# A second layer's merges with tokens as the stationary side and 512 weight columns moving, and a new opening

## The chip, the cores and the metric

The kernel runs on one core of a Trainium2 chip. The metric is the device time of one execution in microseconds (us), as a median over repeated runs. A core has engines with instruction streams of their own: PE (TensorE) multiplies matrices, DVE (VectorE), ACT (ScalarE) and POOL (GpSimd) work element by element, and SP (SyncE) issues most of the transfers from HBM. They wait for each other through semaphores.

## The reference

Two layers of a trunk with parallel branches work on 256 tokens x and 256 context tokens, each of 1024 channels. Cut to what matters:

```python
for l in range(2):
    last = l == 1
    mod_x = sc @ w_mod[l] + b_mod[l]     # sc = silu(c); six pieces of 1024
    mod_h = sh @ w_mod[l] + b_mod[l]     # the same for the context, sh = silu(c_ctx)
    ux = rms_norm(x, norm1_g[l]) * (1 + cx1) + sx1
    uh = rms_norm(h, norm1_g[l]) * (1 + ch1) + sh1
    qa, ka, va, qb, kb, vb, pc, gates = project(ux, w_in[l], ...)   # and of uh
    ya = neighborhood_attention(qa, ka, va, ka_h, va_h, rpb_a[l])
    yb = gqa_block_attention(rope(qb), concat(kb_h, rope(kb)), concat(vb_h, vb))
    yc = multiscale_pool(pc, w_pool[l], pool_scale[l])
    g = sigmoid(gates)                   # three pieces of 1024
    m = g[0] * (ya @ w_br_a[l]) + g[1] * (yb @ w_br_b[l]) + g[2] * (yc @ w_br_c[l])
    x = x + gx1 * (m @ w_out[l])
    u2 = rms_norm(x, norm2_g[l]) * (1 + cx2) + sx2
    x = x + gx2 * ((silu(u2 @ w_ff1[l]) * (u2 @ w_ff3[l])) @ w_ff2[l])
    if not last:
        ...                              # the same for the context tokens h
```

All of it is float32. The second layer needs the context tokens only for keys and values, so from its queries on it works with 256 tokens, the first layer with 512. `ya` and `yb` have 384 channels, `yc` has 256.

## The kernel before

**Products.** Each float32 matrix product is done as three products of a shorter format, from a high and a low part of both sides (`mm3`, L224 to L229: high by high, high by low, low by high). A weight tile of 128 rows and up to 512 columns is loaded raw by SP, ACT copies it into the high part `wh` (L133) and DVE subtracts to get the low part `wl` (L145). The class `Weights` holds 7 raw tiles and 6 of each part, and works some tiles ahead of PE in the order of a list that the jobs make. Tiles marked `whole` aren't split; they are multiplied in whole float32. Activations are kept with channels on the partitions (`xT`, `u`, `y`, `m`), so that a product's result has channels on the partitions again: the weights are the stationary side, the tokens move, 512 or, in the second layer, 256 of them at a time.

**Order.** `program` makes a list of jobs from the string `ORDER`, one letter a job (layer 1 first): P pooling, K, Q, N projections for the attentions, a, b and c the merges of the three branches. Each job is a generator that yields after some products, and at each yield the scheduler `Side` makes one step of attention, pooling or normalization work; a number that such a step yields says how many ticks it stays away. Another `Side` spreads the product of the modulation vectors for later (`w_mod`, on DVE) over the kernel. No engine reorders anything: what is written out is each engine's order.

**The merges.** `merge_job` does 256 channels of one branch: it multiplies `u` (`uh`, `ul`) by the gate's columns of `w_in` over 8 channel tiles, ACT makes the tanh, it waits until the branch's `y` is there, multiplies that by the branch's weights (2 or 3 tiles), and `mix` joins gate and sum on DVE. Four such jobs make a branch, twelve a layer. The last branch, a, splits the sum into the parts of `m`, the moving side of `w_out` (`into_job`, through `pair`). In the second layer both parts of such a merge are products with 256 moving columns.

**The pooling.** `pool_job` projects `pc`; `pool_mix` sums windows of it on POOL, step by step, splits the result and multiplies it on PE into `yc`. Before that product stands `yield 4`.

**The opening.** `first_job` is written by hand. Two pieces of the modulation, the shift (m0) and the scale (m2) of the first 512 channels, are products of the two vectors `sf` with 8 + 8 whole tiles of `w_mod` in `mod_first`; x comes in between in two halves, is squared on ACT and turned on PE (`turn_x`). `norm_rstd` sums the squares on PE and makes 1/rms. Then DVE multiplies `xT` by it for four channel tiles and POOL for the other four (`xr`), and `start_u` makes the parts of `u` from `xr`, scale and shift:

```python
for kt in range(KT):
    xr.append(self.g([P, TOK], name="xr"))
    (nc.vector if kt < 4 else nc.gpsimd).tensor_tensor(xr[kt], self.xT[:, kt, :], self.r0, ALU.mult)
    steps(m, 1)
```

Behind it come half of the first projection (na, channel tiles 0 to 3), two split pieces of the modulation (m1, m3: shift and scale of the other channels), half of the pooling's projection, and then the second halves of both.

## Time and profile before

| | |
|---|---|
| median of 3 runs | 1223.53 us (1223.06 to 1224.26) |
| the profiled execution | 1225.7 us, its span 1223.9 us (1.8 us lie around it) |
| mean granted clock of PE | 0.993 of full speed |
| busy share of the span | PE 98%, PE's weight loads 86%, DVE 75%, ACT 52%, POOL 10% |
| instructions in the trace | 20,258 |
| read from HBM | 183.05 MB, 150 GB/s over the span |

The profile is of one execution, taken by the hardware profiler. A busy share says how much of the span the engine had an instruction at work; loads of weights overlap products on PE. The granted clock is the share of full speed at which PE was allowed to run; it has two levels, 1.2 and 2.4 GHz, shown as 0.5 and 1.0. The waits are told by the instruction that waited and the one whose end released it.

### The profile page before, as it was taken

How to read it: one execution, taken by the hardware profiler on the slowest of the kernel's cores; microseconds unless marked ns; L12 is line 12 of the kernel's file. 1: busy time of each engine (PE TensorE's matmuls, PEld its weight loads, DVE VectorE, ACT ScalarE, POOL GpSimd, SP SyncE). 2: the span in 40 equal slices, each digit the busy share in tenths (PEclk: the TensorE clock that was granted, in tenths of full speed). 3: DMA queues.
4: the chain of work that ended last, by engine and by line, in shares of the span. 5: the costliest groups of instructions: out<-in, count | busy, mean ns of one | idle time of the engine just before them, and what ended most of it. 6: DMA issues, size and time to landing. Idle time of an engine off the chain costs nothing.

```text
span 1223.9 us, 20258 instructions
## 1 busy us (share of the span) xinstructions
PE 1196.1 (98%) x7059; PEld 1058.0 (86%) x7059; DVE 921.4 (75%) x1770; ACT 641.6 (52%) x1393; POOL 127.3 (10%) x177
## 2 busy tenths in 40 slices
PE   7899999999999999999999999999999999999998
PEld 2788889788888988888888888999999999999987
DVE  5867789989898996768566764788778878765654
ACT  4655588666433543333222333456877767655542
POOL 3253110201100000000000000153022100000000
PEclk9899999999999999999999999999999999999999
DMA  8632244335464535555556663334344565666563
GB/s 280 219 84 77 69 146 120 98 104 159 129 199 146 181 104 166 162 159 171 195 184 214 204 206 116 86 106 113 91 118 114 149 193 164 199 182 184 163 194 113
DMA packets 157522, 185.44 MB, mean 152 GB/s; under 512 B 12792, under 2 KB 135532, under 8 KB 157420
## 3 DMA queue, kind: packets, MB, share of 16 engines
q1 hardware_dynamic: 155612, 181.49, 48.1%
q0 software_dynamic: 1808, 2.66, 1.8%
q8 instruction: 55, 0.90, 0.3%
q14 instruction: 47, 0.39, 0.1%
HBM read 183.05 MB, written 1.05 MB: 150 GB/s over the span
## 4 chain that ended last, share of the span: by engine, by line
PE 83%; DVE 5%; ACT 4%; DMA 4%; POOL 2%; issue 1%; SPq 1%; ACTq 0%; DVEq 0%; POOLq 0%
PE acc L227 25%; PE acc L228 25%; PE acc L229 25%; PE y L840 2%; DMA whole<-in_w_mod_dram 2%; PE pt L886 1%; DVE wl L145 1%; DMA mraw<-in_w_mod_dram 1%; ACT wh L133 1%; POOL s L1027 1%; ACT p L829 1%; PE s L863 1%; PE s L864 1%; ACT p L831 1%; DMA raw<-in_w_in_dram 1%
## 5 line engine op out<-in xcount | busy, mean ns | idle before, releaser
L133 ACT ACTIVATE wh<-raw 128x512 fp32r<-128x512 f32 (+2 forms) x512 | 307.7, 612 | 348.5 <-PE acc L228 228.6
L145 DVE TENSOR_TENSOR wl<-raw,wh 128x512 fp32r<-128x512 f32 (+2 forms) x512 | 339.1, 670 | 151.5 <-ACT wh L133 147.7
L227 PE MATMUL acc<-uh,wh 128*128 128x512 f32 (+1 forms) x784 | 279.6, 358 | 2.9 <-ACT gate L1098 1.6
L229 PE MATMUL acc<-uh,wl 128*128 128x512 f32 (+1 forms) x784 | 276.8, 354 | 2.4 <-DVE wl L145 2.4
L228 PE MATMUL acc<-ul,wh 128*128 128x512 f32 (+1 forms) x784 | 277.3, 355 | 0.3
L490 DVE SCALAR_TENSOR_TENSOR macc<-mraw,sf,macc 128x1024 f32<-128x1024 f32 x112 | 144.4, 1294 | 51.0 <-DMA mraw<-in_w_mod_dram 50.9
L227 PEld LDWEIGHTS acc<-uh,wh 128*128 128x128 f32 x784 | 148.7, 190 | 23.6 <-ACT gate L1098 2.0
L229 PEld LDWEIGHTS acc<-uh,wl 128*128 128x128 f32 x784 | 148.6, 190 | 22.9 <-DVE wl L145 2.9
L228 PEld LDWEIGHTS acc<-ul,wh 128*128 128x128 f32 x784 | 149.0, 190 | 20.3 <-DVE ul L579 0.7
L227 PE MATMUL acc<-wh,uh 128*128 128x384 f32 (+1 forms) x304 | 99.6, 329 | 5.0 <-ACT uh L1374 4.4
L228 PE MATMUL acc<-wl,uh 128*128 128x384 f32 (+1 forms) x304 | 97.8, 322 | 0.0
L229 PE MATMUL acc<-wh,ul 128*128 128x384 f32 (+1 forms) x304 | 97.7, 322 | 0.0
L227 PE MATMUL acc<-u,wh 128*128 128x256 f32 x320 | 91.3, 286 | 0.0
L229 PE MATMUL acc<-u,wl 128*128 128x256 f32 x320 | 91.0, 285 | 0.0
L228 PE MATMUL acc<-u,wh 128*128 128x256 f32 x320 | 90.5, 283 | 0.0
L227 PE MATMUL acc<-hh,wh 128*128 128x512 f32 (+1 forms) x216 | 75.9, 351 | 0.0
L229 PE MATMUL acc<-hh,wl 128*128 128x512 f32 (+1 forms) x216 | 75.6, 350 | 0.0
L228 PE MATMUL acc<-hl,wh 128*128 128x512 f32 (+1 forms) x216 | 75.5, 350 | 0.0
L227 PEld LDWEIGHTS acc<-wh,uh 128*128 128x128 f32 x304 | 58.5, 192 | 6.5 <-ACT uh L1374 4.5
L227 PEld LDWEIGHTS acc<-u,wh 128*128 128x128 f32 x320 | 61.4, 192 | 0.6 <-issue 0.2
L229 PEld LDWEIGHTS acc<-u,wl 128*128 128x128 f32 x320 | 61.4, 192 | 0.3 <-issue 0.2
L228 PEld LDWEIGHTS acc<-u,wh 128*128 128x128 f32 x320 | 61.4, 192 | 0.2 <-issue 0.2
(289 smaller groups left out, 2317.0 us busy)
## 6 DMA issues: line engine op xcount, KB each, us to landing
raw<-in_w_ff_dram SPq DMA_DIRECT2D x264, 256.0 KB, 3.0
mraw<-in_w_mod_dram SPq DMA_DIRECT2D x80, 512.0 KB, 4.1
raw<-in_w_in_dram SPq DMA_DIRECT2D x112, 256.0 KB, 2.7
raw<-in_w_in_dram SPq DMA_DIRECT2D x144, 64.0 KB, 2.0
whole<-in_w_mod_dram SPq DMA_DIRECT2D x32, 256.0 KB, 5.4
raw<-in_w_out_dram SPq DMA_DIRECT2D x32, 256.0 KB, 2.8
raw<-in_w_in_dram SPq DMA_DIRECT2D x16, 192.0 KB, 2.4
raw<-in_w_br_c_dram SPq DMA_DIRECT2D x8, 256.0 KB, 2.9
```

The costliest lines, as they stand in the source:

```text
L133: self.nc.scalar.activation(hi[:, :n], self.raw[i][:, :n], AF.Copy)
L145: self.nc.vector.tensor_tensor(lo[:, :n], self.raw[i][:, :n], self.hi[i][:, :n].bitcast(F32), ALU.subtract)
L227: mm(out, st[0], mv[0], start=start, stop=False)
L228: mm(out, st[0], mv[1], start=False, stop=False)
L229: mm(out, st[1], mv[0], start=False, stop=stop)
L490: nc.vector.scalar_tensor_tensor(acc[v], w, c, acc[v], ALU.mult, ALU.add)
L829: nc.scalar.activation(pt, ps, AF.Exp, scale=-1.0, bias=m, accum_out=s[:, 0:1])
L831: nc.scalar.activation(pt, pt, AF.Copy, scale=s[:, 1:2])
L840: mm(o, st, t[:, kt % 2, :], start=kt == 0 and i == 0, stop=kt == n - 1 and i == 1)
L863: nc.tensor.matmul(ps, st, ks[h][0], start=True, stop=False)
L864: nc.tensor.matmul(ps, st, ks[h][1], start=False, stop=True)
L886: nc.tensor.transpose(ps[:, kt * P : (kt + 1) * P], pr[h, qt][:, kt * P : (kt + 1) * P], self.ident)
```

## The change

**The second layer's merges** are done by `merge_tok` instead of `merge_job`: the tokens' parts are stationary (128 tokens a product), and 512 columns of the weights move. A job does 512 channels of a branch for both halves of the tokens, so two jobs make a branch and six the layer. The three branch tiles of a job are fetched before the first of their products. The gates and the sum now have tokens on the partitions, and the sum over the branches is made on DVE alone. It is then turned back on PE, four transposes for 128 tokens and 512 channels, in `turn_m`, which is a step of the scheduler; the first products of `w_out` wait, in the written order, for the turns of the channels that they need. `ORDER` of the second layer has two letters for each branch instead of four, and one merge c in another place. `pool_mix` yields 12 instead of 4 ahead of its product in that layer.

**The opening.** 8 of the 16 whole tiles of `mod_first` become split ones (`mod_first` has four whole tiles and then four split ones for each piece), the scale is now made before the shift, and each result has four rows instead of two. `norm_rstd` comes in the middle of the first piece: its product over the squares first, then the splits of that piece's four tiles and their products, and then its steps on DVE and ACT. `xr` and `start_u` are gone: `norm_u`, which serves the other normalizations, makes `u` from `xT`, scale and 1/rms in one step; its first two steps stand ahead of the wait for the shift. Two of the eight copies of `turn_x` go to ACT. Six products of the pooling's projection stand ahead of the wait for the second half's scale. 16 products of 128 columns with ones (`WARM`) stand near the first transpose. The three transfers of an `na` tile become one.

```diff
-ORDER = ("KrcQcNgcNcbbbbaaaa", "tQPNKccNcNcbbbbaaaa")
+ORDER = ("KrcQcNgcNcbbbbaaaa", "tQPNKcNcNbbaa")
...
+WARM = 8
...
         ps = self.u()
+        for _ in range(WARM):
+            nc.tensor.matmul(ps[:, P : 2 * P], self.ones, self.ones, start=True, stop=True)
         nc.tensor.transpose(ps[:, 0 : 2 * KT], sc[0 : 2 * KT, :], self.ident[0 : 2 * KT, 0 : 2 * KT])
+        warm = self.u("warm")
+        for _ in range(WARM):
+            nc.tensor.matmul(warm[:, 0:P], self.ones, self.ones, start=True, stop=True)
...
+            if h == 1 and k > 1:
+                nc.scalar.activation(self.xT[:, 4 * h + k, :], ps, AF.Copy)
+            else:
+                nc.vector.tensor_copy(self.xT[:, 4 * h + k, :], ps)
+            yield
...
-    def mod_first(self, l, j):
+    def mod_first(self, l, j, nw):
...
-            return TOK, [f], "whole"
+            return TOK, [f], "whole" if kt < nw else "far"
...
-                w = get.__self__.get_whole()
-                nc.tensor.matmul(ps[0:2, :], self.sf[:, kt, :], w, start=kt == 0, stop=kt == KT - 1)
+                if kt < nw:
+                    w = get.__self__.get_whole()
+                    nc.tensor.matmul(ps[0:4, :], self.sf4[:, kt].rearrange("p v h -> p (v h)"), w, start=kt == 0, stop=kt == KT - 1)
+                else:
+                    w = get(TOK, 5)
+                    st = self.S[:, 4 * kt : 4 * kt + 4]
+                    for i in range(2):
+                        nc.tensor.matmul(ps[0:4, :], st, w[i][:, 0, :], start=False, stop=kt == KT - 1 and i == 1)
...
-    def norm_u(self, kts, vs):
+    def norm_u(self, kts, vs, ahead=UA, wait=None):
...
+        if wait:
+            yield wait
...
                 if kind == "na":
-                    for s in range(3):
-                        c0 = 384 * s + P * p
-                        q.dma_start(
-                            out=dst[:, :, s * P : (s + 1) * P],
-                            in_=rows[:, c0 : c0 + P].rearrange("(k p) c -> p k c", p=P),
-                        )
+                    src = rows[:, 0:1152].rearrange("p (s c) -> p s c", c=384)[:, :, P * p : P * (p + 1)]
+                    q.dma_start(out=dst[:, 0, :].rearrange("p (s c) -> p s c", c=P), in_=src)
...
-            yield 4
+            yield 4 if l == 0 else 12
             ps = self.u("pool")
...
+    def merge_tok(self, l, br, h):
...
+        def run(get):
+            nc = self.nc
+            ps = [self.acc() for _ in range(2)]
+            sg = [self.g([P, TOK], name="gate") for _ in range(2)]
+            for kt in range(KT):
+                self.need_u(kt, slice(0, SEQ))
+                w = [x[:, 0, :] for x in get(TOK)]
+                for tt in range(2):
+                    self.mm3(ps[tt], [x[:, tt * P : (tt + 1) * P] for x in self.uu[kt]], w, kt == 0, kt == KT - 1)
+                    if kt == KT - 1:
+                        nc.scalar.activation(sg[tt], ps[tt], AF.Tanh, scale=0.5)
+                    yield
+            want = {(l, "x", br, i) for i in range(nk)}
+            self.side.until(lambda: want <= self.done)
+            pb = [self.acc() for _ in range(2)]
+            ws = [[x[:, 0, :] for x in get(TOK, k)] for k in range(nk)]
+            for tt in range(2):
+                for k in range(nk):
+                    st = [x[:, tt * P : (tt + 1) * P] for x in self.y[br, k]]
+                    self.mm3(pb[tt], st, ws[k], k == 0, k == nk - 1)
+                    if k < nk - 1:
+                        yield
+                t = self.g([P, TOK], name="mix")
+                nc.vector.scalar_tensor_tensor(t, sg[tt], 1.0, pb[tt], ALU.add, ALU.mult)
+                if br != "c":
+                    nc.vector.tensor_tensor(t, self.m0[h, tt], t, ALU.add)
+                self.m0[h, tt] = t
+                if br == "a":
+                    self.side.add(self.turn_m(h, tt, t), first=True)
+                yield
...
+    def turn_m(self, h, tt, t):
+
+        yield 2
+        ps = self.u("mt")
+        for c in range(4):
+            self.nc.tensor.transpose(ps[:, c * P : (c + 1) * P], t[:, c * P : (c + 1) * P], self.ident)
...
-    def start_u(self, kts):
...
-            m = m0[1](get)
+            ws._dma(2 * KT + 4)
+            m = m2[1](get)
             steps(m, X0)
             steps(self.turn_x(x0, 0), 9)
             steps(m, X1)
             steps(self.turn_x(x1, 1), 9)
+            ws._dma(4 * KT + 4)
+            self.norm_rstd(slice(0, TOK), lambda: (ws._lo(KT), steps(m, 4)))
             steps(m, 9)
-            m = m2[1](get)
             steps(self.turn_rows, 9)
-            self.norm_rstd(slice(0, TOK))
-            xr = self.xr = []
-            for kt in range(KT):
-                xr.append(self.g([P, TOK], name="xr"))
-                (nc.vector if kt < 4 else nc.gpsimd).tensor_tensor(xr[kt], self.xT[:, kt, :], self.r0, ALU.mult)
-                steps(m, 1)
-                if kt == 3:
-                    ws._lo(ws.n_whole + 4)
+            m = m0[1](get)
+            steps(m, 1)
+            self.side.until(lambda: ("mod", 0, 2) in self.done)
+            steps(m, 3)
+            ws._lo(2 * KT)
+            ws._hi(2 * KT + 1)
+            self.side.add(self.norm_u(range(4), (0, 1), 2, lambda: ("mod", 0, 0) in self.done), first=True)
...
-            self.side.add(self.start_u(range(4)), first=True)
...
             steps(m3[1](get), 99)
+
+            self.side.until(lambda: ("mod", 0, 1) in self.done)
+            steps(p, 1)
             self.side.until(lambda: ("mod", 0, 3) in self.done)
-            self.side.add(self.start_u(range(4, KT)), first=True)
+            self.side.add(self.norm_u(range(4, KT), (0, 1)), first=True)
...
-        return m0[0] + m2[0] + wa[:4] + m1[0] + m3[0] + wp[:2] + wa[4:] + wp[2:], run
+        return m2[0] + m0[0] + wa[:4] + m1[0] + m3[0] + wp[:2] + wa[4:] + wp[2:], run
...
             for br in "abc":
-                made[br] = iter([self.merge_job(l, T, br, jp) for jp in range(4)])
+                if last:
+                    made[br] = iter([self.merge_tok(l, br, h) for h in range(2)])
+                else:
+                    made[br] = iter([self.merge_job(l, T, br, jp) for jp in range(4)])
```

In the opening, on DVE, from the first `xr` of before and from the first piece of the modulation in the change (`ut` is `xT` by scale and 1/rms, `modt` the turned result of a piece, `whole` and `raw` are weight tiles as loaded). Before:

```order
L1415 TENSOR_TENSOR xr_336<-xT,rstd_117 128x512
L1415 TENSOR_TENSOR xr_339<-xT,rstd_117 128x512
L1415 TENSOR_TENSOR xr_342<-xT,rstd_117 128x512
L449 COPY mod_110<-modt_345 128x8
L453 TENSOR_TENSOR mod_110<-mod_110,cols_109 128x8
L145 TENSOR_TENSOR wl_354<-raw_190,wh_352 128x384
L145 TENSOR_TENSOR wl_358<-raw_194,wh_356 128x384
L145 TENSOR_TENSOR wl_362<-raw_198,wh_360 128x384
L145 TENSOR_TENSOR wl_366<-raw_202,wh_364 128x384
L449 COPY mod_110<-modt_382 128x8
L453 TENSOR_TENSOR mod_110<-mod_110,cols_109 128x8
L519 SCALAR_TENSOR_TENSOR A_111<-mod_110,cols_109 128x8
```

And with the change:

```order
L469 TENSOR_REDUCE mod_130<-modt_366 128x8
L471 TENSOR_TENSOR mod_130<-mod_130,cols_129 128x8
L537 SCALAR_TENSOR_TENSOR A_131<-mod_130,cols_129 128x8
L146 TENSOR_TENSOR wl_379<-whole_202,wh_377 128x512
L146 TENSOR_TENSOR wl_383<-whole_204,wh_381 128x512
L146 TENSOR_TENSOR wl_387<-whole_206,wh_385 128x512
L146 TENSOR_TENSOR wl_391<-whole_208,wh_389 128x512
L590 SCALAR_TENSOR_TENSOR ut_395<-xT,A_131,rstd_137 128x256
L590 SCALAR_TENSOR_TENSOR ut_397<-xT,A_131,rstd_137 128x256
L146 TENSOR_TENSOR wl_399<-raw_210,wh_393 128x384
L469 TENSOR_REDUCE mod_130<-modt_411 128x8
L471 TENSOR_TENSOR mod_130<-mod_130,cols_129 128x8
```

The scale `A` stood behind the four `xr` and the four splits of the projection's weights; it now stands ahead of the four splits of the second piece, two `ut` stand ahead of the shift's reading, and no `xr` is left.

On PE, at the same place in the program, the gate part of a merge early in the second layer: the accumulators are `acc`, the moving side stands first behind the arrow and the stationary side second, `uh` and `ul` are parts of `u`, `kt` is a transpose of the attention's keys. Before:

```order
L707 MATMUL kt_8989<-ident,zkn_8913 128x128 x2
L707 MATMUL kt_8989<-ident,zkn_8914 128x128 x2
L227 MATMUL acc_8997<-uh_8093,wh_8799 128x256
L228 MATMUL acc_8997<-ul_8094,wh_8799 128x256
L229 MATMUL acc_8997<-uh_8093,wl_8801 128x256
L227 MATMUL acc_8997<-uh_8095,wh_8799 128x256
L228 MATMUL acc_8997<-ul_8096,wh_8799 128x256
L229 MATMUL acc_8997<-uh_8095,wl_8801 128x256
L707 MATMUL kt_9014<-ident,zkn_8913 128x128 x2
L707 MATMUL kt_9014<-ident,zkn_8914 128x128 x2
L227 MATMUL acc_8998<-uh_8093,wh_8799 128x256
L228 MATMUL acc_8998<-ul_8094,wh_8799 128x256
```

And with the change:

```order
L725 MATMUL kt_8976<-ident,zkn_8900 128x128 x2
L725 MATMUL kt_8976<-ident,zkn_8901 128x128 x2
L228 MATMUL acc_8984<-wh_8778,uh_8105 128x512
L229 MATMUL acc_8984<-wl_8780,uh_8105 128x512
L230 MATMUL acc_8984<-wh_8778,ul_8106 128x512
L725 MATMUL kt_8998<-ident,zkn_8900 128x128 x2
L725 MATMUL kt_8998<-ident,zkn_8901 128x128 x2
L228 MATMUL acc_8985<-wh_8778,uh_8105 128x512
L229 MATMUL acc_8985<-wl_8780,uh_8105 128x512
L230 MATMUL acc_8985<-wh_8778,ul_8106 128x512
L228 MATMUL acc_8984<-wh_8786,uh_8107 128x512
L229 MATMUL acc_8984<-wl_8824,uh_8107 128x512
```

Between the same two pairs of transposes stood six products, two channel tiles with 256 moving tokens; now it is three products, one channel tile with 512 moving weight columns.

On PE, at the change from the last merge to `w_out` (before: `y` are the branch's parts, `m` the sum's; with the change `mix` is the sum, `mt` its turn, `mh` and `ml` its parts). Before:

```order
L229 MATMUL acc_11548<-y_10999,wl_11490 128x256
L227 MATMUL acc_11549<-y_10999,wh_11476 128x256
L228 MATMUL acc_11549<-y_10999,wh_11476 128x256
L229 MATMUL acc_11549<-y_10999,wl_11490 128x256
L227 MATMUL acc_11592<-m_11214,wh_11494 128x256
L228 MATMUL acc_11592<-m_11214,wh_11494 128x256
L229 MATMUL acc_11592<-m_11214,wl_11508 128x256
```

And with the change:

```order
L228 MATMUL acc_11070<-mh_10890,wh_11014 128x256
L229 MATMUL acc_11070<-ml_10891,wh_11014 128x256
L230 MATMUL acc_11070<-mh_10890,wl_11026 128x256
L228 MATMUL acc_11183<-mh_10887,wh_11080 128x256
L229 MATMUL acc_11183<-ml_10888,wh_11080 128x256
L1211 MATMUL mt_11104<-ident,mix_11066 128x128 x4
L230 MATMUL acc_11183<-mh_10887,wl_11082 128x256
L228 MATMUL acc_11183<-mh_10887,wh_11080 128x256
L229 MATMUL acc_11183<-ml_10888,wh_11080 128x256
L230 MATMUL acc_11183<-mh_10887,wl_11082 128x256
L228 MATMUL acc_11069<-mh_11055,wh_11030 128x256
```

The last product of the merges was followed at once by `w_out`; now four transposes of the last sum stand among products of `w_out` that take the parts turned earlier, and the products on the parts behind that turn follow from `mh_11055` on.

## Rows read from the trace of the kernel before

**Rows 1.** The page, part 1: busy time, share of the span, instructions

```profile
PE 1196.1 (98%) x7059; PEld 1058.0 (86%) x7059; DVE 921.4 (75%) x1770; ACT 641.6 (52%) x1393; POOL 127.3 (10%) x177
```

**Rows 2.** Waits of PE: who for whom, us in total, times, longest

```profile
PE acc L227 <- ACT uh L1374: 4.4, 1, 4.4
...
PE acc L227 <- ACT gate L1098: 2.1, 3, 1.4
PE pool L227 <- ACT plh L237: 1.8, 1, 1.8
```

**Rows 3.** Stretches of the opening: busy us and instructions by engine, clock, DMA

```profile
28.97:33.40 4.43, 0.00 (x0) 0.00 (x1) 3.66 (x11) 0.65 (x2) 3.02 (x4) 0.98 1.00 326
33.40:36.40 3.00, 3.00 (x9) 2.59 (x10) 2.90 (x8) 3.00 (x7) 0.00 (x0) 0.50 1.15 363
36.40:43.60 7.20, 7.20 (x41) 7.00 (x41) 6.68 (x15) 3.33 (x6) 4.84 (x11) 0.99 0.85 282
...
51.50:53.40 1.90, 1.03 (x10) 0.70 (x9) 1.90 (x5) 1.86 (x5) 0.00 (x0) 1.00 0.23 31
53.40:57.00 3.60, 3.60 (x10) 2.87 (x10) 3.26 (x11) 1.09 (x2) 0.00 (x0) 0.54 0.92 292
```

**Rows 4.** Timeline of the opening: start, us, engine, line, operation, count, wait before

```profile
14.19 0.63 ACT L317 ACTIVATE sq<-xin 128x512 f32<-128x512 f32 x1
...
14.57 2.48 DVE L322 COPY xT<-acc 128x512 f32<-128x512 f32 x4 [2.32 <-PE acc L321]
...
17.25 0.87 DVE L328 TENSOR_SCALAR ssq<-ident,ss 128x128 f32<-128x128 f32 x4
...
20.42 3.59 PE L406 MATMUL mod<-whole,sf 128*2 128x512 f32 x8
...
22.78 0.69 DVE L550 SCALAR_TENSOR_TENSOR rstd<-rs,rstd 128x512 f32<-128x512 f32 x1
...
23.51 5.71 DVE L1415 TENSOR_TENSOR xr<-xT,rstd 128x512 f32<-128x512 f32 x4
...
30.29 1.95 DVE L145 TENSOR_TENSOR wl<-raw,wh 128x384 fp32r<-128x384 f32 x4
...
33.40 0.69 PE L227 MATMUL acc<-wh,uh 128*128 128x384 f32 x1 [4.43 <-ACT uh L1374]
```

**Rows 5.** The tile xr: ns min, median, max of its group on DVE

```profile
L1415 DVE TENSOR_TENSOR xr<-xT,rstd x4: 691/1748/1756, 23.5 to 27.5; 128x512 f32<-128x512 f32 x4
```

**Rows 6.** Timeline: prices of DVE steps, and the opening's last pool product

```profile
424.17 1.27 DVE L570 SCALAR_TENSOR_TENSOR ut<-xT,A,rstd 128x256 f32<-128x256 f32 x3
...
44.54 6.71 DVE L145 TENSOR_TENSOR wl<-whole,wh 128x512 fp32r<-128x512 f32 x11 [0.73 <-ACT wh L133]
...
74.13 0.39 PE L229 MATMUL y<-uh,wl 128*128 128x512 f32 x1
```

**Rows 7.** Timeline of PE: runs of 256 and of 512 columns

```profile
1076.01 0.28 PE L228 MATMUL acc<-u,wh 128*128 128x256 f32 x1
...
1079.97 0.28 PE L228 MATMUL acc<-u,wh 128*128 128x256 f32 x1
...
1166.05 0.39 PE L227 MATMUL acc<-wh,h 128*128 128x512 f32 x1
...
1171.94 0.39 PE L229 MATMUL acc<-wh,h 128*128 128x512 f32 x1
```

**Rows 8.** Timeline of PE: four transposes, and what follows them

```profile
870.55 0.60 PE L886 MATMUL pt<-ident,p 128*128 128x128 f32 x4
...
870.91 0.42 PE L227 MATMUL acc<-wh,uh 128*128 128x384 f32 x1
```

**Rows 9.** The second layer's pooling: a POOL step, and a stretch behind it

```profile
813.07 7.09 POOL L1027 TENSOR_TENSOR s<-vp 128x271 f32<-128x271 f32 x1
...
824.00:829.00 5.00, 4.92 (x22) 4.78 (x22) 5.00 (x9) 3.26 (x10) 1.49 (x2) 0.66 0.26 72
```

**Rows 10.** The stretch of the second layer's merges

```profile
840.00:1003.00 163.00, 159.43 (x1237) 155.14 (x1237) 132.24 (x331) 124.06 (x304) 22.07 (x30) 1.00 0.45 125
```

More of the change, by code (lines that the diff above doesn't have):

```diff
@@ L543, in norm_rstd @@
         self.tc.keep_in_program_order(mm)
+        if between:
+            between()
         av, t = (self.g([P, TOK], name="rs")[:, c] for _ in range(2))
@@ L570, in normed @@
                 nc.vector.scalar_tensor_tensor(ts[i], self.xT[:, kt, c], g, self.r0[:, c], ALU.mult, ALU.mult)
-        for i in range(UA):
+        for i in range(ahead):
             normed(i)
+        if wait:
+            yield wait
         for i, (kt, c, v) in enumerate(todo):
@@ L622, in run @@
             for i0 in range(0, nu, per):
-                ws = [get(cols, i) for i in range(per)]
+                ws = [get(cols, i + 3 * (fresh and i0 == 0)) for i in range(per)]
                 todo = [(i, k, tt) for tt in range(ntt) for i in range(per) for k in range(kpu)]
@@ L985, in pair @@
                         self.need_u(kt, sl)
+                    if rhs is self.m and self.mp:
+                        need = {("m", kt // 4, tt) for tt in range(2)}
+                        if not need <= self.done:
+                            self.side.until(lambda: need <= self.done)
                     self.mm3(
@@ L1451, in layer_start @@
         self.y, self.m0, self.m, self.h = {}, {}, [], []
+        self.mp = {}
         self.gain = self.g([P, 2, HD], name="gain")
```

69 lines of the change are left out of this document (44 added, 25 removed).

## The prediction

> **What bounds the kernel now.** I read the page's busy times first: TensorE (PE) is busy for 98% of the span [rows 1], so what counts is PE's idle time and the pace of its products; the other engines matter where PE waits for them. The list of waits, for PE alone, comes next [rows 2]: its longest is 4.4 us for the first `uh` tile, the others that this change touches are 1.8 us for `plh` in the second layer's pooling, and 2.1 us in three waits for `gate` in its merges. The stretches of the opening [rows 3] show the first of them whole: from 28.97 to 33.40 PE does nothing, then 3.0 us run at a granted clock of 0.50 (the lower level, 1.2 GHz), and after a second pause (1.03 of 1.90 us busy up to 53.40) most of the next 3.6 us does so again. The timeline says what was late [rows 4]: the last piece of x is squared from 14.19 on, `rstd` is ready at 22.78 + 0.69 = 23.5, and then VectorE (DVE) needs 5.71 us for four `xr` products, 1.95 us for four `wl`, and only then makes the scale `A`, so that the first projection product stands at 33.40. DVE's `xr` take 1.75 us in the median where the fastest takes 0.69 [rows 5]; GpSimd (POOL) makes the other four at the same time.
>
> **The change part by part: the opening.** I walk the new order with durations from rows of before. The loads are the same tiles in the same order up to x, so the squares end as now, at 14.19 + 0.63 and a read-out, near 15.0. The sums follow at once (0.87 us for four [rows 4], and a small step), 16.0; two of the four copies into `xT` (0.62 each, 2.48 for four [rows 4]) end on DVE at 17.3, the other two go to ScalarE (ACT). Now the new work: eight of the sixteen `w_mod` tiles are split into high and low parts. In a row DVE takes 0.61 us per `wl` (6.71 for 11) [rows 6]; ACT's `wh` run ahead of it. The first four `wl` end at 19.9, the three steps of `rstd` (0.7 each) at 22.0, the columns and the scale's small steps near 22.9, four more `wl` at 25.4, two `ut` (0.42 each, 1.27 for three [rows 6]) and one `wl` of 384 columns (0.49, 1.95 for four [rows 4]) at 26.7. PE's part of this hides behind DVE: four plain products of a group take 3.59 us now [rows 4], and the eight split ones of the shift end with the last `wl`, near 25.8 to 26.1; the row of results goes through ACT and four small transposes (some 1.2 us with DVE's two small steps), and the shift is there at about 27.3. One `uh` later, **27.9 instead of 33.40**, the first projection product starts: 5.5 us. What goes away is the 5.71 us of `xr` and the fresh scale and shift behind it; what is paid for it is 8 x 0.61 us of `wl`, half of them where DVE waits for `rstd` now.
>
> From 27.3 DVE is again what PE waits for: 14 steps of `ut` and `ul` (5.9 us), three `wl` of 384 (1.5) and sixteen of 512 (9.8) end at 44.5. The scale and shift of the second half end with them, and the six pool products that now stand ahead of the second turn hide that turn's way through ACT. With one more `wl` the pool products start near 45.2 instead of 53.40. Then 48 products of 512 columns at 0.2265 [rows 7], 48 of 384 at 0.176 (7.20 us for 41 [rows 3]) and a turn of 0.4 follow without a pause if the clock stays at its upper level: 45.2 + 19.7 = 64.9; before, the last of them starts at 74.13 [rows 6] and ends its turn at 74.4. That is 9.5 us; I take **9.2**, because for kt 4 to 7 two `ut`, two `ul` and a `wl` (2.2 us) stand against 2.1 us of products, which leaves no slack. Bounds: 6.5, if both stretches at clock 0.50 return (3.0 and 3.6 us at half speed, some 3 us in all), and 11, if DVE keeps its shortest times. The merged `na` loads (one DMA for three) ask SP for fewer issues; no wait of PE hangs on them now, so they count as nothing, and if they do bring weights sooner, DVE is still what is waited for. From the second turn on, the order of PE is that of before, product by product, until the second layer's pooling, so nothing should be given back there.
>
> **The second layer's merges.** 768 products with 256 columns become 384 with 512. In a run of 33 steps the former follow each other every 0.120 us, in a run of 26 the latter every 0.2265 [rows 7]: 92.2 against 87.0 us, a gain of 5.2. The sum has to be turned back: 16 transposes in four groups, 0.36 us each (870.55 to 870.91 [rows 8]), +1.4. The last turn is behind the last merge: mix and add on DVE, PE, ACT. The order puts 26 products of `w_out` (3.1 us) ahead of the turn and five more behind it, while two DVE steps and one of ACT, none of more elements than a `wl` of 0.61 us, need 2; I count nothing, and up to 1.5 us if DVE's queue is late there. The pooling's products move past a third of a chunk (some 6 us). They are now late because POOL's first addition takes 7.09 us there [rows 9]; that wait of 1.8 us goes, and with it, I think, the stretch behind it at a mean clock of 0.66 over 5 us [rows 9], which costs 5 x 0.34 = 1.7. Of the 2.1 us of waits for `gate` I take half, since there are six hand-overs instead of twelve and a longer branch part covers each. Against this: DVE is busy for 132 and ACT for 124 of the 163 us of this stretch [rows 10]; in 155 us the same work fills DVE to 85%, and in the new order the scores start some 12 us later but end only 5 to 6 us later (products counted in the order, at the paces of rows 7), so the attention's share of ACT and DVE work is packed some 6% closer. I charge 2.5 us of new waits (none to 6). Sum: -5.2 + 1.4 - 1.8 - 1.7 - 1.0 + 2.5 = **-5.8 us**.
>
> The pace is where a rule of the Trainium skill speaks against the change. Its page "TensorE: Matmul & The Clock Gate", section "Back-to-back issue gap", puts an isolated product at N / 2.4 + 2.5 ns. By that the 768 would cost 84.0 and the 384 83.0 us, an estimate from that page, and the sum of gain and transposes would be a loss of 0.4 instead of a gain of 3.8 us. The trace agrees for neither width.
>
> **Sum.** -9.2 - 5.8 = -15.0 us. On the profiled execution, 1225.7 us (a span of 1223.9 and 1.8 around it), that is 1210.7; the median of the runs shown is 2.2 lower, so I predict **1208.5 us**.
>
> **The rivals.** (a) *The merges give nothing back but the pooling's wait:* ACT and DVE, packed closer, hold PE up in each of six jobs by about 0.9 us, so the 5.8 shrink to 0.4. For it: three waits for `gate` already, the longest of 1.4 us [rows 2]; against it: fewer and longer jobs. 1213.9. (b) *512 columns are no cheaper per column inside the merges*, where transposes and scores break the runs of 256 anyway and loads of weights hide: then only 1.4 us of transposes are left of that term, and the layer gives 0.6: 1213.7. This is how the page's rule would show itself. Rows 7 come from unbroken runs, so it isn't excluded, but most merge products stand in runs of six and more at 0.12. (c) *The opening waits elsewhere:* the shift's last split or the load of its tiles is late by 3 us, PE is left idle again and both stretches at clock 0.50 return; 9.2 becomes 4: 1213.7. Against it: the last group of eight pieces runs from 20.42 in 3.59 us, so PE finds its tiles there now [rows 4]. (d) *Slower:* a merge now takes three branch tiles at once and holds them, so the splits of the next job begin late; a wait at each of twelve changes between gate and branch parts. It decides from 1.25 us each (15.0 / 12); at the longest `gate` wait of today, 1.4 [rows 2], the time would be 1225.3. Against it: DVE needs 0.61 us for a tile that feeds six products of 0.2265, 1.36 us.
>
> **How the numbers follow.** Chances: forecast 0.64, (a) 0.13, (b) 0.08, (c) 0.12, (d) 0.03. The forecast's own bounds (opening 6.5 to 11, second layer 2.3 to 8.5) reach from 1204 to 1214.7 if both lie at one end; the rivals (a) to (c) lie at 1213.7 to 1213.9. The range **1202.5 to 1214.5** holds the forecast's bounds but for their corners, and leaves some mixes of rivals and (d) above. A measurement of this kernel tells 0.2% (2.4 us) from no change; all cases but (d), and a mix of (a) and (c) at 1219, are far below, so faster 0.95, same 0.02, slower 0.03.
>
> **What would show it.** In the new profile: the first projection product near 27.9 and the last pool product near 65; no stretch at clock 0.5 in the first 70 us; `xr` gone and no DVE group above 0.7 us ahead of `uh`; in the merges products of 512 columns every 0.2265 us; no PE wait for `plh` and a clock of 1.00 around the second pooling; at most 1.5 us between the merges and `w_out`. I am wrong in the opening if PE still stands idle for over 3 us before the first product, and in the second layer if PE's waits from the first merge to `w_out` add up to over 6 us.

## The result, and the profile after

The changed kernel takes **1217.24 us** (median of 4 runs, 1215.92 to 1218.11) against 1223.3 us before on the same chip (4 runs): a ratio of 0.9948, 95% interval 0.9936 to 0.996. Measured again beside some of the experiments it was 0.9963 (0.9951 to 0.9975). By the two ratios the gain is 4.5 to 6.4 us; 15 were forecast, and the time lies above the range.

The page of the changed kernel, its busy times, which answer to [rows 1]:

```profile
span 1215.7 us, 19294 instructions
...
PE 1192.6 (98%) x6707; PEld 1036.6 (85%) x6707; DVE 918.3 (76%) x1757; ACT 641.3 (53%) x1387; POOL 112.1 (9%) x166
```

The waits of PE in it (who for whom, us in total, times, longest), which answer to [rows 2]:

```profile
PE acc L228 <- DVE v L240: 4.4, 4, 2.6
...
PE kt L725 <- DVE zkn L801: 1.6, 2, 1.0
...
PE acc L228 <- ACT uh L599: 1.0, 1, 1.0
...
PE modt L464 <- ACT mrow L427: 0.7, 1, 0.7
```

The wait of 4.4 us for `uh` has shrunk to 1.0 and the wait for `plh` is gone, as forecast; those for `gate` are gone too, of which the forecast took half. But there is a new one of 2.6 us for `v`, and it stands only 24 products, 3.5 us of PE's work, behind the place where the wait for `plh` was. The timeline of the opening (start, us, engine, line, operation, count, wait before) answers to [rows 4] and [rows 6]:

```profile
15.80 0.63 ACT L326 ACTIVATE sq<-xin 128x512 f32<-128x512 f32 x1
...
29.95 0.69 PE L228 MATMUL acc<-wh,uh 128*128 128x384 f32 x1 [1.01 <-ACT uh L599]
...
40.13 4.28 ACT L134 ACTIVATE wh<-whole 128x512 fp32r<-128x512 f32 x8 [1.43 <-PE acc L230]
...
40.79 6.71 DVE L146 TENSOR_TENSOR wl<-whole,wh 128x512 fp32r<-128x512 f32 x11 [1.21 <-ACT wh L134]
...
48.33 0.50 PE L228 MATMUL pool<-uh,wh 128*128 128x512 f32 x1
...
68.08 0.39 PE L230 MATMUL y<-uh,wl 128*128 128x512 f32 x1
```

The last piece of x is squared at 15.80 instead of 14.19, the first projection product stands at 29.95 (forecast 27.9), the first pool product at 48.33 (45.2) and the last starts at 68.08 (64.9 was forecast for its end, 74.13 before). In the merges of the second layer a run of 512-column products, the timeline of PE, beside [rows 7]:

```profile
837.52 0.39 PE L229 MATMUL acc<-wl,uh 128*128 128x512 f32 x1
...
843.19 0.39 PE L230 MATMUL acc<-wh,ul 128*128 128x512 f32 x1
```

25 steps lie between them: 0.2268 us each, the pace of the forecast in an unbroken run. What the merges cost as a whole is added up further down. Where the time went differently shows in four stretches of the timelines:

| us, from the timelines | before | change | change again |
|---|---|---|---|
| last square of x starts | 14.19 | 15.80 | 15.81 |
| last pool product of the opening | 74.13 | 68.08 | 68.09 |
| from there to layer two's first `ss` product | 711.06 | 711.81 | 711.52 |
| from there to its first product on `xh` (the FFN) | 243.49 | 240.75 | 241.07 |

In these traces the opening gives 6.0 instead of 9.2, some is given back on the way, and the second layer gives 2.4 to 2.7 instead of 5.8. One thing more is needed to read single traces: executions of one kernel differ by some 3 us with the granted clock. Beside one group of the experiments, 14 runs of the kernel before took 1221.5 to 1222.6 us where the mean clock was 0.997 and 1223.1 to 1225.3 where it was 0.994; the profiled one of before had 0.993 and 1225.7.

### The profile page after: what moved, and what is told of

It reads as the page before. It is cut to its first block, busy times and chain, and to the rows that moved or that the text cites. A ratio compares the mean times of both kernels' runs of the same rounds, so it can differ in the third digit from the quotient of the medians.

```text
span 1215.7 us, 19294 instructions
## 1 busy us (share of the span) xinstructions
PE 1192.6 (98%) x6707; PEld 1036.6 (85%) x6707; DVE 918.3 (76%) x1757; ACT 641.3 (53%) x1387; POOL 112.1 (9%) x166
## 4 chain that ended last, share of the span: by engine, by line
PE 83%; DVE 6%; ACT 4%; POOL 3%; DMA 2%; issue 2%; SPq 0%; ACTq 0%; DVEq 0%; POOLq 0%
PE acc L228 24%; PE acc L229 24%; PE acc L230 24%; PE y L858 2%; PE pt L904 1%; DVE wl L146 1%; POOL s L1049 1%; ACT wh L134 1%; DMA mraw<-in_w_mod_dram 1%; PE s L881 1%; DVE macc L508 1%; PE s L882 1%; DMA xin<-in_x_dram 1%; ACT p L847 1%; PE mod L446 1%
## 5 line engine op out<-in xcount | busy, mean ns | idle before, releaser
L134 ACT ACTIVATE wh<-raw 128x512 fp32r<-128x512 f32 (+1 forms) x508 | 306.4, 615 | 350.4 <-PE acc L229 213.5
L146 DVE TENSOR_TENSOR wl<-raw,wh 128x512 fp32r<-128x512 f32 (+1 forms) x508 | 336.4, 671 | 153.6 <-ACT wh L134 150.6
L228 PE MATMUL acc<-uh,wh 128*128 128x512 f32 (+1 forms) x592 | 223.4, 379 | 1.4 <-DVE v L240 1.4
L230 PE MATMUL acc<-uh,wl 128*128 128x512 f32 (+1 forms) x592 | 222.2, 377 | 2.4 <-DVE wl L146 2.4
L228 PE MATMUL acc<-wh,uh 128*128 128x384 f32 (+2 forms) x400 | 137.3, 344 | 4.0 <-DVE v L240 3.0
L229 PE MATMUL acc<-wl,uh 128*128 128x384 f32 (+2 forms) x400 | 134.9, 338 | 0.0
L230 PE MATMUL acc<-wh,ul 128*128 128x384 f32 (+2 forms) x400 | 134.8, 337 | 0.0
L229 PEld LDWEIGHTS acc<-wl,uh 128*128 128x128 f32 x400 | 76.2, 190 | 3.9
L230 PEld LDWEIGHTS acc<-wh,ul 128*128 128x128 f32 x400 | 75.9, 190 | 3.8
L228 PEld LDWEIGHTS acc<-u,wh 128*128 128x128 f32 x320 | 61.4, 192 | 0.6 <-issue 0.2
```

The source lines that it names most:

```text
L134: self.nc.scalar.activation(hi[:, :n], self.raw[i][:, :n], AF.Copy)
L146: self.nc.vector.tensor_tensor(lo[:, :n], self.raw[i][:, :n], self.hi[i][:, :n].bitcast(F32), ALU.subtract)
L228: mm(out, st[0], mv[0], start=start, stop=False)
L229: mm(out, st[0], mv[1], start=False, stop=False)
L230: mm(out, st[1], mv[0], start=False, stop=stop)
```

## The experiments

**The parts alone.** First the two halves of the change, each with the other as before; then a repeat of the change as it is.

```diff
 open_only: the change, but
+ORDER = ("KrcQcNgcNcbbbbaaaa", "tQPNKccNcNcbbbbaaaa")   # merge_job in both layers, yield 4
 merge_only: before, but
+ORDER = ("KrcQcNgcNcbbbbaaaa", "tQPNKcNcNbbaa")         # merge_tok, turn_m, yield 12
```

> The new opening with the second layer as it was before. Reading of the two traces: the last pool product of the opening starts 6.0 us earlier, and 0.9 of that is given back by 225 us, so about 1218.2 us (5.1 less than before). The prediction's own term, if the opening was only spoilt by the merges: 9.2 less, 1214.1.

> The new merges, their order and the later pooling product, with the opening as it was. Reading of the two traces: 2.7 us less than before if the stretch at clock 0.66 near 825 us stands in most runs of before (1220.6), 1.0 less if it was an accident of the profiled run (1222.3). The prediction's own term: 5.8 less, 1217.5.

Measured: open_only 0.9976 (0.9966 to 0.9985), some 2.9 us; merge_only 0.9977 (0.9967 to 0.9988), 2.8 us. The two add up to the change, so neither spoils the other: each part is itself half or a third of what was forecast. For open_only the 5.1 us expected from one pair of traces was too much as well: its last pool product came at 68.43, but from there to the second layer it took 713.22 us.

> The changed kernel once more, unaltered, beside the three below on one chip: 0.9948 of before (0.9936 to 0.996), some 6.3 us less. Its second trace tells which waits recur: theory: the first projection product between 29.4 and 31.6 us, as in the four traces with the new opening so far, a wait for ptl near 180 us of 0.5 to 1.7 us, and a wait of 2.6 us for v near 820 us. Rival, for the last two: they were accidents of one execution and are gone.

The table above shows it: the numbers of the opening recur within 0.02 us, the wait for `v` too (2.61 us at 822.55), and that for `ptl` comes again, longer (1.58 us at 179.52, 0.62 at 178.54 in the first trace). The 0.02 us are luck, though. In the six traces that have this same opening (the change, change_again, open_only, and pool4, late_split and dve_pool below) the last square starts between 15.2 and 16.5 us, the first projection product between 29.4 and 32.0, and the last pool product between 67.4 and 70.3, 68.7 in the mean. Three traces with the opening of before have the last pool product at 73.4, 73.4 and 74.1 (merge_only, before_dve, before). In the means the opening therefore gives 4.9 us, not 6.0.

**Where the wait for `plh` went.** In the changed kernel, the timelines of POOL, DVE, ACT and PE around the place, and ahead of them one of the five other places of POOL's step:

```profile
74.61 0.64 POOL L1049 TENSOR_TENSOR s<-vp 128x271 f32<-128x271 f32 x1
...
807.78 7.09 POOL L1049 TENSOR_TENSOR s<-vp 128x271 f32<-128x271 f32 x1
...
814.02 0.35 DVE L779 TENSOR_TENSOR rot<-zqn,rope 128x192 f32<-128x192 f32 x1
...
818.48 0.42 DVE L240 TENSOR_TENSOR pll<-r,plh 128x256 fp32r<-128x256 f32 x1 [4.11 <-ACT plh L238]
...
818.03 0.42 ACT L238 ACTIVATE plh<-r 128x256 fp32r<-128x256 f32 x1 [4.45 <-POOL r L1075]
...
822.83 0.39 PE L228 MATMUL acc<-wh,uh 128*128 128x256 f32 x1 [2.59 <-DVE v L240]
```

POOL's first addition takes 7.09 us, so `r` is late; ACT stands 4.45 us at `plh` and DVE 4.11 at `pll`. Behind these two, in the same queues, stand the split tiles and the `v` of the attention, whose accumulator PE needs next. The change moved PE's product only. Two runs move something else:

```diff
 pool4: the change, but in pool_mix
-            yield 4 if l == 0 else 12
+            yield 4
 late_split: the change, but in pool_mix
-                yield 2
+                yield 2 if l == 0 else 8
                 self.split(...)                          # plh, pll
-            yield 4 if l == 0 else 12
+            yield 4 if l == 0 else 6
```

> The changed kernel with 4 instead of 12 ahead of the pooling's product in the second layer. Theory: the stall is in the queues of ACT and DVE, which wait for POOL at plh and pll wherever PE's product stands, so PE waits 1.8 us for plh instead of 2.6 for v, and the time stays within 1 us of the changed kernel's (1216.2 to 1218.2). Prediction's step: the later place was worth 3.5 us, so 1220.7.

> The changed kernel, in whose second layer also the splits plh and pll of the pooling stand later (8 ticks instead of 2, the product then 6 later instead of 12), behind the first v in the queues of ACT and DVE. Theory: then nothing waits for POOL's 7.1 us step, PE's wait of 2.6 us for v goes, and the time is 2 to 2.6 us less than the changed kernel's, 1214.6 to 1215.2. Rival: POOL's late result is waited for further down, or DVE has no room for the splits there: within 0.7 us of 1217.2.

Measured: pool4 0.9955 (0.9941 to 0.9968), no slower than the change; in its trace PE waits 1.76 us for `plh` again, and the second layer takes 239.85 us, 0.9 less than with the product moved. late_split: 0.9918 (0.9903 to 0.9932), some 4 to 5 us less than the change, and 237.81 us for the layer: the wait for `v` is down to 1.55, and of the waits for `zkn`, 1.6 us in the trace of the change (in change_again there were none), none is left. So the stall was in the queues of ACT and DVE, and moving the product of PE brought nothing.

Why POOL takes 7.09 us for an addition that takes 0.64 to 0.99 us in the other five of its six places shows in late_split, where DVE has more to do before its first pause:

```profile
807.94 9.24 POOL L1049 TENSOR_TENSOR s<-vp 128x271 f32<-128x271 f32 x1
...
816.12 0.56 DVE L825 TENSOR_TENSOR zqn<-zqn,rot 128x384 f32<-128x384 f32 x1
817.28 2.30 DVE L146 TENSOR_TENSOR wl<-raw,wh 128x512 fp32r<-128x512 f32 x2 [0.60 <-ACT wh L134]
```

DVE pauses at 816.68 (816.12 + 0.56) and POOL's step ends at 817.18; in the change DVE pauses at 814.37 and POOL ends at 814.87. In all thirteen traces that have this step on POOL it ends 0.50 us after DVE's first pause; in before_dve below, where the second group's first addition meets a shorter row of DVE, it takes 3.49 us and ends 0.49 after the pause. The Trainium skill names a cause, in "SBUF — State Buffer", sections "Terms" and "Who interferes with whom": a DVE instruction with two SBUF inputs and a GpSimd instruction that reads SBUF contend for a pair of ports, which one of them holds for its whole instruction. The trace agrees and goes further: here POOL waits out an unbroken row of DVE instructions, 7 and 9 us long, not one. That it waits for DVE is shown by the lengths; that it waits for the ports is the page's reading, which no run here tells from another. Two runs take the step away from POOL:

```diff
 dve_pool: the change, before_dve: the kernel before, but in pool_mix
+            eng = nc.vector if (l, c) == (1, 0) else nc.gpsimd   # for the five steps of group c
```

> The changed kernel with the second layer's first group of pooling steps (channels 0 to 127) on DVE instead of POOL. Theory: POOL's first addition takes 7.1 us because DVE works without a break for that time (in ten traces it ends 0.5 us after DVE's first pause); on DVE the five steps take some 2 us of a queue that stands idle for 4 us behind them, plh follows at once, and PE's wait of 2.6 us for v and the clock's fall behind it go: 2.6 to 3.5 us less than the changed kernel's, 0.9925 to 0.9935 of before. Rival: DVE's queue then is what is late, and PE waits there for v or wl as long as now: 0.9955.

> The kernel before with the same five steps on DVE. Theory: the stall is no matter of the merges; PE's wait of 1.8 us for plh goes, and in about half of the runs the stretch at half clock behind it: 1.8 to 3 us less than before, 0.9975 to 0.9985. What dve_pool has over this kernel is then the change without the stall. Rival: another wait takes its place: 1.0.

Measured: dve_pool 0.9935 (0.9923 to 0.9948), before_dve 0.9981 (0.9971 to 0.9991), with 238.97 and 241.07 us for the second layer. Both kernels gain about 2 us from it (before_dve 2.3 by its ratio, dve_pool 1.6 or 3.4, set against the one or the other ratio of the change), so the stall has nothing to do with the merges; without it the merges are worth 241.07 - 238.97 = 2.1 us in this pair of traces. Some of the stall stays in both: PE waits 1.25 us in dve_pool for another `v`, where the second group of pooling steps is on POOL, and 1.06 us in before_dve for `pll`.

**What the merges cost as a whole.** The same two traces have no stretch at the lower clock in this layer. Added up from the start of one product of PE to the start of the next, without the waits that the timeline shows, they give:

| us, from layer two's first `ss` product to its first on `xh` | before_dve | dve_pool |
|---|---|---|
| products of the merges (768 and 384) | 95.3 | 92.0 |
| turns of the sum (16 transposes) | - | 1.5 |
| products and transposes of the attention | 35.7 | 36.6 |
| products of `w_out` | 23.1 | 23.4 |
| all other products | 82.2 | 82.3 |
| PE's waits | 4.8 | 3.2 |

So the wider products saved 3.3 us, not 5.2, and with the turns and the slower neighbours only 0.5 us are left of the 3.8 that were forecast for products and turns. The other 1.6 us come from waits, where the forecast had 1.5 us more. The pace of the forecast holds inside the runs, but the attention's products break them some 50 times. Behind a transpose a product costs 0.08 to 0.09 us more than in a run, at either width:

```profile
979.84 0.63 PE L1211 MATMUL mt<-ident,mix 128*128 128x128 f32 x4
980.22 0.47 PE L229 MATMUL acc<-wl,y 128*128 128x512 f32 x1
980.54 0.39 PE L230 MATMUL acc<-wh,y 128*128 128x512 f32 x1
```

These are from the change: 0.32 from start to start where a run has 0.2268. With the other joints such extras come to 3.3 us in before_dve and 5.0 in dve_pool; why the 512-column products pay more there was not tested. The four other traces with the old merges give the same sum for their products within 0.1 us, and ten of the eleven others with the new ones within 0.2 (pool4, whose order of products differs, is 1.2 lower).

**Why the opening starts late.** x came 1.6 us later, though SP issues it as before. What is new is on POOL's own queue:

```profile
4.67 0.60 POOL L1504 DMA_DIRECT2D cst<-in_cst_dram  x1
5.26 0.55 POOL L1541 DMA_DIRECT2D gain<-in_q_norm_b_dram  x1
5.80 0.53 POOL L1541 DMA_DIRECT2D gain<-in_k_norm_b_dram  x1
```

Before, these loads (416 KB for `cst`) stood behind POOL's four `xr`, which waited for 1/rms, and were issued at 30.3 us. With `xr` gone nothing holds them, and they run beside the second half of x: a transfer of x takes 8.6 us to land in the change and 7.0 in the kernel before (medians of the pages). The first run below holds the loads back, the second fills PE's pauses instead.

```diff
 late_cst: the change, but in first_job
+            nc.gpsimd.tensor_copy(self.small(1, "hold"), self.r0[:, 0:1])
             nc.gpsimd.dma_start(out=self.cst, in_=self.a["cst"])
 warm_gap: the change, but in mod_turn, for the first shift
+        for _ in range(10): nc.tensor.matmul(pt[:, P : 2 * P], self.ones, self.ones, start=True, stop=True)
...
+        for _ in range(14): nc.tensor.matmul(keep[:, 0:P], self.ones, self.ones, start=True, stop=True)
```

> The changed kernel with one small copy on POOL that reads 1/rms ahead of the loads of cst, gain and wpool, so that these are issued near 23 us, as before the change, instead of at 4.7 us. Theory: they took bandwidth from x; without them the last square starts near 14.2 instead of 15.8 us, the first projection product stands near 28.4 us, and the time is 1.5 us less than the changed kernel's. Rival: x is late because the transfers of x and of w_mod take each other's bandwidth, whatever POOL does: first product within 0.5 us of the changed kernel's, same time.

> The changed kernel with 10 products of 128 columns with ones between the last product of the shift and its turn on PE, and 14 behind the turn, where PE stands idle for 0.7 and 1.0 us. Theory: the stretch at half clock from 30 to 33.3 us comes from these pauses; with PE at work in them the clock stays at its upper level and the last pool product of the opening comes 1.6 us earlier: 1.6 us less than the changed kernel's. Rival: the clock falls for what PE did earlier (few rows of output in the products of w_mod), and still falls: same time, or 0.3 us more for the added products.

late_cst: 0.9941 (0.9929 to 0.9953), 2.7 us less than the change beside it, with intervals that barely overlap, and in its trace, ACT and PE:

```profile
13.56 0.63 ACT L326 ACTIVATE sq<-xin 128x512 f32<-128x512 f32 x1
...
27.71 0.44 PE L228 MATMUL acc<-wh,uh 128*128 128x384 f32 x1 [1.01 <-ACT uh L599]
```

With the loads held back x is there 0.6 us earlier than before the change, and the first projection product stands at 27.71, where 27.9 was forecast. All other traces agree: the last square starts at 13.6 to 14.4 us in the five with the loads held back and at 13.8 to 14.2 in the four with the old opening, but at 15.2 to 16.5 in the eight others. warm_gap: 0.9966 (0.9954 to 0.9979), the time of the change. Its clock stayed up in the opening, but that shows nothing, since it stayed up in five of twelve traces of the new opening without those products too. What it does show, together with them, is that the fall near 30 us costs nothing. Stretches of the change and of na3 (below): PE, PEld, DVE, ACT, POOL busy (instructions), granted clock, DMA:

```profile
30.00:35.00 5.00, 5.00 (x20) 4.98 (x21) 5.00 (x13) 4.53 (x11) 0.00 (x0) 0.67 1.04 381
```

```profile
30.00:35.00 5.00, 4.62 (x25) 4.06 (x25) 5.00 (x13) 4.53 (x11) 0.00 (x0) 1.00 0.97 310
```

At 0.67 PE is busy throughout, at 1.00 it waits, and DVE is busy for all 5 us in both. From the first projection product to the last pool product it takes 38.13 us in the one and 38.09 in the other, and 38.1 to 38.6 in all seven traces with the fall, 38.1 to 38.7 in the five without. An earlier fall is another matter: in late_split and dve_pool the clock was also at 0.50 for 3.4 us from 16 us on, and there the way from the last square to the first projection product took 15.4 and 15.5 us, where the ten others took 14.1 to 14.3.

**What is given back later.** In nine of ten traces with one transfer for an `na` tile PE waits 0.5 to 1.7 us for `ptl` near 180 us, in none of the seven with three. These runs tell the transfer from the opening:

```diff
 na3: the change, but for an na tile, as before
+                    for s in range(3):
+                        c0 = 384 * s + P * p
+                        q.dma_start(
...
 before_na1: the kernel before, but with one, as in the change
+                    src = rows[:, 0:1152].rearrange("p (s c) -> p s c", c=384)[:, :, P * p : P * (p + 1)]
```

> The changed kernel with three transfers for an na tile, as before the change. Theory: the single transfer shifts the loads behind it in SP's queue, and the wait for ptl near 180 us (0.5 to 1.7 us, after a late mraw) comes from that; with three it goes, and the delta to before at 190 us is that of 70 us: about 1 us less than the changed kernel's. Rival: the wait is the price of standing 5 us earlier beside transfers that take as long as before, and stays; the opening may lose up to 0.5 us by the longer issues: 0 to 0.5 us more.

> The kernel before with one transfer instead of three for an na tile, and nothing else. If the single transfer makes the wait for ptl by itself: the wait stands near 185 us with 0.5 to 1.7 us, the way from the opening's last pool product to the second layer takes some 711.6 us instead of 710.0 (means of nine and five traces so far), and the time is 0.5 to 1.6 us more than before, 1.0004 to 1.0013. Rival: it takes the new opening's earlier phase too, and here there is no such wait: 1.0.

na3: 0.9947 (0.9935 to 0.996), 1.9 us less than the change beside it, with intervals that overlap, and without the wait. before_na1: **1.0021** (1.0011 to 1.0031), 2.6 us slower than before, more than expected. Its wait, the timelines of SP, DVE and PE:

```profile
176.99 0.38 SPq L943 DMA_DIRECT2D raw<-in_w_in_dram  x1
177.46 1.29 SPq L463 DMA_DIRECT2D mraw<-in_w_mod_dram  x1
...
182.69 1.28 DVE L490 SCALAR_TENSOR_TENSOR macc<-mraw,sf,macc 128x1024 f32<-128x1024 f32 x1 [1.00 <-DMA mraw<-in_w_mod_dram]
...
186.31 0.63 PE L924 MATMUL pt<-ident,p 128*128 128x128 f32 x4 [1.10 <-DVE ptl L239]
```

In the kernel before, the same tile is issued at 172.06 and the same `mraw` at 175.27. With one transfer they go out 5 and 2 us later (0.9 of it is this trace's later opening), `mraw` lands late, DVE stands before it, and `ptl` is behind DVE. One `na` transfer takes 2.7 us to land, one of the three 2.0 (medians of the two pages). The first projection product of before_na1 is late too, 34.54 against 33.40. How the single transfer makes the loads behind it wait for a later `wl` wasn't settled.

The way from the opening's last pool product to the second layer tells the price, if traces are compared that have equally many stretches at the lower clock there (near 217, 417 and 438 us):

| stretches at 0.50 on the way | one transfer, us | three transfers, us |
|---|---|---|
| none | 710.0 to 710.2 (3 traces) | 708.7 to 709.7 (3) |
| one | 710.9 to 713.2 (4) | 709.9 (1) |
| two | 712.6 to 714.0 (3) | 711.1 to 712.6 (3) |

The single transfer costs 1.0 us in the first row and 1.4 in the last, by the means. Two stretches go with 2.6 and 3.0 us more. So the first table of this document's results flatters the change on this way: its trace has one stretch at 0.50 here, that of before has two.

**Together.** Which repairs add up:

```diff
 both: the change + late_cst + dve_pool
 all_na3: both + na3
 open_fixed: open_only + late_cst + na3
 final: the change + late_cst + na3 + late_split
```

> The changed kernel with the late loads of cst and with the pooling steps on DVE. If both theories hold and add up: 1.8 and 2.6 to 3.5 us less than the changed kernel's, 0.991 to 0.992 of before. If the opening's gain is taken back by a wait near 180 us again: 0.9925.

> The kernel of the run both, with three transfers for an na tile as well. If the single transfer makes the wait for ptl near 180 us: no such wait here, and 0.5 to 1 us less than both. If that wait comes by chance: the same time as both.

> The new opening alone, second layer as before, with the late loads of cst and three transfers for an na tile. Theory: the two together are what the opening lost against the 9.2 us of the prediction, but for 1.1 us of DVE's wait behind ACT between the first projection and the pool products: last pool product near 66.0 us, 8.1 less than before, and 7.5 to 8 us less in time, 0.9935 to 0.994 of before (the opening alone had 0.9976). Rival: the later waits for transfers take back what comes earlier: 0.996 or more.

> The change with the late loads of cst, three transfers for an na tile, and the pooling's splits later in the queues (late_split) instead of its steps on DVE. By the traces the second layer takes 237.8 us with late_split and 238.9 with the steps on DVE, so 1.1 us less than all_na3: 0.990 of before. Rival: the splits' place and the other two get in each other's way: 0.991 to 0.992.

Measured: both 0.9925 (0.9912 to 0.9937), the upper of its two numbers, with a wait of 0.59 us for `ptl`; all_na3 0.9911 (0.9897 to 0.9924), without it, with intervals that overlap; open_fixed 0.9955 (0.9943 to 0.9966), 5.5 us, between its two: the last pool product comes at 66.74, 7.4 us earlier than in the trace of before; final 0.9911 (0.9898 to 0.9924), 10.9 us less than before, the rival's number. Its second layer takes 237.74 us, as expected, but that does not show in the time against all_na3.

## Why the prediction was wrong, step by step

**The opening, "the squares end as now".** This step failed first. The same tiles came in the same order on SP, but POOL's queue was left out: without `xr` its loads come 26 us sooner and take bandwidth from x. It cost 1.6 of the 2.0 us at the first projection product, and late_cst gives it back. The steps between took 14.15 us in both, 13.7 were forecast. Of the 9.2 us the opening gave 4.9 in the means, and 7.0 in the five traces with the loads held back (last pool product at 66.6).

**"Again what PE waits for" is DVE, 17.3 us to the pool products.** 18.4 were measured, and 18.9 in late_cst. DVE's steps have the lengths assumed; missing is a wait of 1.21 us for `wh`, which ACT makes late because it waits 1.4 us for PE to free a tile (the waits of ACT in this stretch). The splits were summed as if their buffers were endless. The last part, 19.7 us to the end, was nearly right (19.75 to the start of the last product, 19.98 to its end).

**The clock at 0.50.** The forecast that no such stretch would return was wrong, and so was its price of some 3 us for two: the first returned in seven of twelve traces and costs nothing there, because DVE is the bound. For the second pooling 1.7 us was the price: 240.75 us without the stretch (change) and 241.07 with it (change again), 0.3; the waits for `zkn` that follow in the one are gone in the other. A slow stretch was priced by itself, without asking what PE waits for next. Not every stretch is free, though: those near 217 and 438 us go with 1.3 to 1.5 us each (the table of the stretches above).

**"Count as nothing": the merged na loads.** They cost. 2.6 us in the kernel before, 1.0 to 1.4 us between the opening and the second layer with equally many stretches at the lower clock, and that is also why "nothing should be given back there" failed.

**"That wait of 1.8 us goes, and with it the stretch behind it": -3.5.** It brought nothing. The wait went to `v`, 2.6 us, because the splits of the same pooling block ACT and DVE. What would be late next was asked of PE's queue and not of the two queues that make its operands. POOL's 7.09 us were read as its own length, and it was DVE's.

**Products, transposes, gates, new waits: -5.2 + 1.4 - 1.0 + 2.5 = -2.3.** Right as a sum, 2.1 us between before_dve and dve_pool, but by luck: two terms were wrong by some 3 us, in opposite directions. Products and turns gave 0.5 instead of 3.8, since the paces of unbroken runs were taken for merges that are broken some 50 times. The waits became 1.6 us less instead of 1.5 more: all 2.1 us for `gate` and one of 1.1 for `p` went, and 1.6 us for `zkn` came. Of the 2.5 us of new waits that denser work on ACT and DVE was to bring, those for `zkn` are all that came.

**The rivals.** None as told. (c) had the size of the opening's loss, "the opening waits elsewhere", but named the shift's tiles instead of x; (a) was nearer than the forecast in the second layer (0.4 us left of 5.8, against 2.4), but PE's waits there are not spread over six jobs: over half of them stand at one stall that the change leaves as it is. (b) is refuted for unbroken runs by the pace of 0.2268, but it was partly right for the merges, of whose 5.2 us 3.3 came. (d) is refuted by the absence of waits at the twelve changes.

**The signs of being wrong.** Neither showed: PE stood idle for 1.0 us right before the first projection product, not 3, and its waits in the second layer add up to 5.0 us in the change, not 6. Both asked for waits of PE, and the largest losses were x that came late, a stall that had been there before, and products that cost more at their joints.

**Two slips in its sums** change nothing: the formula that it takes from the Trainium skill, "TensorE: Matmul & The Clock Gate", section "Back-to-back issue gap", gives an estimate of 83.8 and 82.9 us for the 768 and 384 products, not 84.0 and 83.0, and the second layer's upper bound of 8.5 is 8.3 by its own terms.

## What to carry to other kernels

When work is taken off an engine, list what stands behind it in that engine's queue, transfers above all: they start sooner and collide with something. A stalled operand is cured at its maker: moving the consumer helps only if the maker's queue holds nothing else that is needed meanwhile. A slow clock or a wait is worth only what the next wait behind it leaves over. And a pace read from an unbroken run is a bound for work that others break: count the joints, or add up the same stage in a trace.

## What was not expected of the hardware

- POOL's addition of 128x271 took 7.09 to 9.24 us beside an unbroken row of DVE instructions, and 0.64 to 1.04 us nearly everywhere else; it ended 0.50 us after DVE's pause in each of thirteen traces.
- The same wait is followed by a stretch at the lower clock in some executions and not in others: after the 1.5 us for `pth` near 217 us in ten of seventeen traces, after the 2.4 us for `wl` near 438 us in five of them. Two such stretches between the opening and the second layer go with 2.6 to 3.0 us more.
- One transfer of 192 KB in place of three of 64 KB made the kernel slower by 0.21% (0.11 to 0.31).
